# Four moved pieces in a two-block transformer kernel: which weight quarter is loaded first, when gated results are transposed, when the seven-product blocks start, and which PSUM banks the mixers' transposes use

## The chip, the cores and the metric

One core of one Trainium2 chip runs the whole program. The metric is the device time of one execution in microseconds. The kernel before took 1137.19 us (median of 3 runs, 1135.1 to 1139.62).

## What is computed

Two transformer blocks on 256 tokens of width 1024, all in float32. Each block is a SwiGLU feed-forward network (FFN) of inner width 2816, a mixer (sparse attention with pooling in the first, spatial gating with short convolution in the second), and another FFN; a last normalisation follows. The part that the change touches most is the FFN, of which there are four:

```python
def swiglu(x, w_gate, w_up, w_down):
    return (jax.nn.silu(x @ w_gate) * (x @ w_up)) @ w_down

x = x + 0.5 * swiglu(rms_norm(x, ffn1_norm[l]), ffn1_w_gate[l], ffn1_w_up[l], ffn1_w_down[l])
x = x + mixer(rms_norm(x, mix_norm[l]))          # attention and pooling, or gating and convolution
x = x + 0.5 * swiglu(rms_norm(x, ffn2_norm[l]), ffn2_w_gate[l], ffn2_w_up[l], ffn2_w_down[l])
```

## The kernel before

**Products in three passes.** Each float32 operand is split into a high half (ACT, a rounding copy, L77) and a low half (DVE, the remainder, L78), and a product is three matmuls, high x high, low x high and high x low (`mm3`, L83 to L85). Every weight chunk of 128x2048 thus goes from a buffer in which a transfer lands (`raw`, two buffers, filled by SP's queue, L67; or `block`, four buffers in an FFN, filled by Pool's queue, L151) through ACT and DVE into one of three pairs `whi`/`wlo`, and then to TensorE (PE).

**An FFN's steps.** The gate and up weights are cut into pieces of 512 columns, j = 0 to 5 (piece 5 holds 256 columns of each). Pieces 0, 2, 4 and 5 take the plain way (`eight`, L344): a step is one chunk of 1 MB from SP's queue and 24 matmuls for the two token tiles. Piece 5 has two steps (letter e), pieces 2 and 4 four each (letters 2 and 4). Pieces 1 and 3 (`seven`, L358, with `quad`, L154) replace eight block products by seven: letters a and b, seven steps of 12 matmuls each. Below, a1 is the first step of a, 2.1 the first of piece 2, and so on. The `down` steps (letter d) take 24 matmuls (12 for chunk 5), in the order of chunks 0, 1, 2, 4, 5, 3 for the first half of the columns. The string `ORDER` is the order in which the steps are written into the program, for all four FFNs.

**The seven products.** `quad` loads four quarters w11, w12, w22 and w21 of the piece through Pool's queue. Step a2 wants w12+b22 and step a5 wants w11+b12. The sums are made by the transfer itself: a second transfer with `accum_op=add` (L175) goes into the same buffer. For w12 it waits until the first transfer has landed; for w11 also until a1's halves are made. For a6 and a7, DVE adds w22 and w21 to that block (L192, L195). Pool's queue is in order: a transfer whose buffer is not free holds up those behind it. The block buffers w22 and w21 get are those in which DVE combines the activations beforehand (`combined`, L133); the second of them is free only when the combined activations `xc` have been split.

**Work that is put off.** When a piece's gate and up results are done, DVE multiplies them into `pr` (L338), and `turned` (L204) transposes `pr` on PE (L210) and splits it into `act`, which the down steps read. `later(f, n)` keeps such a piece of work until n units have passed; `flush` after a step counts 1 unit for a step of a or b and 2 for any other (L408). With n = 2, `turned` comes right after the step that ended the piece (for piece 0, right after the next step).

**PSUM.** Of the eight banks five are called `acc` and three `tmp`. `bank` takes the next buffer of one name in turn; `ps` (L58) goes through all eight. In the mixers most tiles come from `ps`, but `turned` and the transposes of the next stage's input (`pair`, L266) take `tmp`. `spare` is true in the mixers alone.

A scheduler orders the instructions on each engine; the code order is its input.

Of the kernel before, what the change touches and what calls it, by code (L numbers as in the profile page):

```python
# [17 lines left out]
P = 128  # L18
T = 256
# [13 lines left out]
MASKED = -1.0e30  # L33
WARM = 14

ORDER = "eaeaa2a2aa2a244bb4bb4bdbdbdddddddddd"


class Block:
# [14 lines left out]

    def bank(self, tag, shape=(P, 512)):
        return self.psum.tile(list(shape), F32, tag=tag, name=tag, bufs={"acc": 5, "tmp": 3}[tag])

    def ps(self, shape=(P, 512)):  # L58
        self.banks += 1
        return self.bank("acc" if self.banks % 8 < 5 else "tmp", shape)  # L60
# [93 lines left out]
    def quad(self, pool, b, x, xc):  # L154


        nc, tt = self.nc, self.nc.vector.tensor_tensor
        of_x = lambda c, t: lambda k: self.both(x[:, 4 * c + k, :, t * P : t * P + P])
        of_xc = lambda i: lambda k: self.both(xc[:, 4 * i + k, :, :])

        def product(left, w):
            ps = self.bank("tmp")
            for k in range(4):
                c = slice(k * 512, k * 512 + 512)
                self.mm3(ps, left(k), (w[0][:, c], w[1][:, c]), k == 0, k == 3)
            return ps

        p = lambda tag: pool.tile([P, 512], F32, tag=tag, name=tag)

        def copy(ps, tag):  # L170
            y = p(tag)
            nc.scalar.activation(y, ps, AF.Copy)
            return y

        more = lambda w, src: nc.gpsimd.dma_start(w, src, accum_op=ALU.add)  # L175
        (b11, b12), (b21, b22) = b
        w11, w12, w22, w21 = self.block(b11), self.block(b12), self.block(b22), self.block(b21)
        more(w12, b22)
        y11 = copy(product(of_x(0, 0), self.parts(w11)), "p1")
        more(w11, b12)  # L180
        yield
        p7 = copy(product(of_xc(2), self.parts(w12)), "p7")
        yield
        y12 = copy(product(of_xc(3), self.parts(w22)), "p3")
        yield
        y21 = p("p2")
        tt(y21, product(of_x(1, 0), self.parts(w21)), y11, op=ALU.add)
        y11, v = y21, y11
        yield
        p5 = copy(product(of_xc(0), self.parts(w11)), "p5")  # L190
        yield
        tt(w11, w11, w22, op=ALU.add)  # L192
        tt(v, product(of_xc(1), self.parts(w11)), v, op=ALU.subtract)
        yield
        tt(w11, w11, w21, op=ALU.add)  # L195
        w = self.parts(w11)
        ps = product(of_x(1, 1), w)
        tt(p7, p7, v, op=ALU.add)
        tt(v, v, p5, op=ALU.add)
        tt(p5, p7, p5, op=ALU.add)  # L200
        tt(p7, ps, p7, op=ALU.subtract)
        return y11, p7, y12, v, p5

    def turned(self, dst, x, k):  # L204

        for t in range(2):
            n = x[t].shape[1] // P
            pt = self.bank("tmp", (P, 4, P))
            for i in range(n):
                self.nc.tensor.transpose(pt[:, i, :], x[t][:, i * P : i * P + P], self.ident)  # L210
            s = slice(t * P, t * P + P)
            self.split(dst[:, k : k + n, 0, s], dst[:, k : k + n, 1, s], pt[:, :n, :])
# [37 lines left out]
    def add(self, accs, f, scale, following, tiles=(0, 1)):  # L250

        nc = self.nc
        s = slice(f * 512, f * 512 + 512)
        for t in tiles:
            x = self.X[t][:, s]
            nc.vector.scalar_tensor_tensor(x, accs[t], scale, x, op0=ALU.mult, op1=ALU.add)
        if following is None:
            return
        for t in tiles:
            self.squares(t, f)  # L260
        if following == "final_norm_2":
            return
        if f == 0:
            self.hT = self.big.tile([P, KD, 2, T], F32R, tag="hT", name="hT")

        def pair(k):  # L266
            pt = self.bank("tmp", (P, 2, T))
            for i in range(2):
                for t in range(2):
                    nc.tensor.transpose(pt[:, i, t * P : t * P + P], self.X[t][:, (k + i) * P : (k + i) * P + P], self.ident)  # L270
            for i in range(2):
                self.feed(k + i, pt[:, i, :], following)

        for k in (4 * f, 4 * f + 2):
            self.later(lambda k=k: pair(k), 3)
# [42 lines left out]
    def ffn(self, n, following, first=False):  # L318
        nc, a = self.nc, self.a
        gu, d, d_end = a[f"gu{n}"], a[f"d{n}"], a[f"de{n}"]  # L320
        with self.stage(4), self.tc.tile_pool(name="act", bufs=1) as pool:
            act = pool.tile([P, KF, 2, T], F32R, tag="act", name="act")
# [11 lines left out]
            def gated(j, sgs, us):  # L334
                prs = []
                for t in range(2):
                    pr = self.work.tile([P, 512], F32, tag="pr", name="pr", bufs=4)[:, : us[t].shape[1]]
                    nc.vector.scalar_tensor_tensor(pr, us[t], r[:, t : t + 1], sgs[t], op0=ALU.mult, op1=ALU.mult)  # L338
                    prs.append(pr)
                self.later(lambda: self.turned(act, prs, 4 * j), 2)  # L340

            two = lambda: [self.bank("acc") for _ in range(2)]

            def eight(j):  # L344
                G = two()
                self.token_major(G, gu[2 * j], 512, 0)
                yield
                self.token_major(G, gu[2 * j], 512, 1)
                sgs = silu([x[:, :T] for x in G] if j == 5 else G)
                if j < 5:  # L350
                    yield
                    U = two()
                    self.token_major(U, gu[2 * j + 1], 512, 0)
                    yield
                    self.token_major(U, gu[2 * j + 1], 512, 1)
                gated(j, sgs, [x[:, T:] for x in G] if j == 5 else U)

            def seven(j):  # L358
                y11, y21, y12, x, y22 = yield from self.quad(pool, [[gu[2 * j + i, c] for i in range(2)] for c in range(2)], self.hT, xc)

                def rest():
                    tt = nc.vector.tensor_tensor
                    tt(y12, y12, x, op=ALU.add)
                    gated(j, silu([y11, y21]), [y12, y22])

                self.later(rest, 3)

            def down():
                for f in range(2):
                    accs = two()  # L370
                    w = lambda c: self.weights(d[f, c] if c < 5 else d_end[f])
                    rows = lambda c, w, last, **k: self.rows(accs, w, act, 4 * c, 4 if c < 5 else 2, last, **k)
                    split = f == 1 and following == "final_norm_2"
                    order = (0, 1, 2, 4, 5, 3) if f == 0 else range(4 if split else 6)
                    for c in order:
                        if f or c:
                            yield
                        rows(c, w(c), 15 if f == 0 else KF - 1)
                    if split:
                        ws = [w(4), w(5)]  # L380
                        for t in range(2):
                            for c in (4, 5):
                                rows(c, ws[c - 4], KF - 1, tiles=[t])
                            self.add(accs, f, 0.5, following, [t])
                    else:
                        self.add(accs, f, 0.5, following)
# [12 lines left out]
            if not first:  # L399
                self.token_major(U, gu[1], 512, 1)  # L400
            gated(0, silu(G), U)
            combined = self.combined(xc, self.hT)
            next(combined)

            steps = {"a": seven(1), "b": seven(3), "2": eight(2), "4": eight(4), "e": eight(5), "d": down()}
            for step in ORDER:
                next(steps[step], None)
# [34 lines left out]
    def mixer1(self, following):  # L442
# [225 lines left out]
        def out(t, O):  # L668
# [4 lines left out]
            self.split(mT[0][:, :, 0, s], mT[0][:, :, 1, s], pt)  # L673

        ET = turned(0)
        pls = means()
        O = attend(0, ET)
        pooled(pls)
        ET = turned(1)
        mT[0] = self.m1.tile([P, 4, 2, T], F32R, tag="L1", name="mT")  # L680
        project(1, 0)
# [281 lines left out]
```

## Time and profile before

| what | value |
|---|---|
| median of 3 runs | 1137.19 us (1135.1 to 1139.62) |
| profiled execution, its own time | 1135.03 us |
| its span, first to last instruction | 1133.3 us |
| PE busy | 1081.6 us, 95% of the span |
| DVE busy | 758.3 us, 67% |
| ACT busy | 576.0 us, 51% |
| mean granted TensorE clock | 0.983 of full speed |
| DMA engines' mean busy share, first two queues | 39.8% and 16.1% |

The profile comes from one execution. "Busy" counts instructions of an engine; the waits are in a view that says, for each group of instructions, what ended the idle time before them. The granted clock says at which of its two levels (1.2 and 2.4 GHz) TensorE ran in a stretch.

### The profile page before, as it was taken

Reading aid. Unit: us, or ns where it says so; the run is one execution under the profiler, and the core shown is the slowest. Engines: PE = TensorE matmul, PEld = TensorE weight load, DVE = VectorE, ACT = ScalarE, POOL = GpSimd, SP = SyncE. Lnnn points to the kernel's source line nnn. Section 1 sums busy time; section 2 is a strip of 40 time slices with the busy share of each in tenths; the row PEclk is TensorE's granted clock in tenths of the full one; section 3 lists DMA queues with packets and bytes.
Section 4 is the critical chain, followed back from the end, with each engine's and each line's share of the span. In section 5 each row is a group of like instructions: output and inputs, shape, how many; then the busy total and the mean of one; then the engine's idle time right before and its main releaser. Section 6 shows DMA issues by size and latency. Waiting matters only on the chain.

```text
span 1133.3 us, 12907 instructions
## 1 busy us (share of the span) xinstructions
PE 1081.6 (95%) x5182; PEld 900.8 (79%) x5182; DVE 758.3 (67%) x780; ACT 576.0 (51%) x657; POOL 51.2 (5%) x85
## 2 busy tenths in 40 slices
PE   9898999899998899999889999999999999889996
PEld 7677888778887688888768878999888878767885
DVE  6685875597575769646776855687545557666953
ACT  7545543577454464544646454533444445546442
POOL 1100000120010000001000000000000001000000
PEclk9999999999998999999989999999999999999999
DMA  9956365633386743659574565454545438674362
GB/s 355 284 176 226 112 231 187 251 112 113 112 290 192 259 115 132 224 188 313 179 260 112 206 229 208 175 189 174 184 176 178 169 120 281 201 253 119 130 223 74
DMA packets 34956, 218.54 MB, mean 193 GB/s; under 512 B 4609, under 2 KB 5009, under 8 KB 10321
## 3 DMA queue, kind: packets, MB, share of 16 engines
q1 hardware_dynamic: 26784, 164.20, 39.8%
q0 software_dynamic: 7680, 52.98, 16.1%
q8 instruction: 40, 0.66, 0.2%
q10 hardware_dynamic: 432, 0.55, 0.1%
q14 instruction: 20, 0.16, 0.0%
HBM read 216.66 MB, written 1.05 MB: 192 GB/s over the span
## 4 chain that ended last, share of the span: by engine, by line
PE 70%; DVE 10%; DMA 10%; issue 5%; ACT 4%; POOL 0%; SPq 0%; POOLq 0%; ACTq 0%; DVEq 0%
PE acc L85 16%; PE acc L83 16%; PE acc L84 16%; PE tmp L83 6%; PE tmp L84 6%; PE tmp L85 6%; DVE wlo L78 6%; DMA block<-in_gu 5%; DMA raw<-in_gu 4%; ACT whi L77 3%; PE tmp L210 2%; PE acc L91 1%; DMA raw<-in_d 1%; DVE xc L78 1%; DVE block L192 1%
## 5 line engine op out<-in xcount | busy, mean ns | idle before, releaser
L78 DVE TENSOR_TENSOR wlo<-raw,whi 128x2048 fp32r<-128x2048 f32 (+1 forms) x127 | 282.2, 2222 | 175.4 <-ACT whi L77 175.4
L77 ACT ACTIVATE whi<-raw 128x2048 fp32r<-128x2048 f32 (+1 forms) x127 | 236.3, 1860 | 244.3 <-PE acc L85 106.8
L78 DVE TENSOR_TENSOR wlo<-block,whi 128x2048 fp32r<-128x2048 f32 (+2 forms) x99 | 198.5, 2013 | 100.4 <-ACT whi L77 100.3
L85 PE MATMUL acc<-whi,hT 128*128 128x512 f32 (+1 forms) x608 | 238.1, 392 | 3.2 <-DVE hT L223 3.2
L83 PE MATMUL acc<-whi,hT 128*128 128x512 f32 (+1 forms) x608 | 240.0, 396 | 0.5 <-ACT whi L77 0.4
L84 PE MATMUL acc<-wlo,hT 128*128 128x512 f32 (+1 forms) x608 | 238.4, 392 | 1.3 <-DVE wlo L78 1.3
L77 ACT ACTIVATE whi<-block 128x2048 fp32r<-128x2048 f32 (+2 forms) x99 | 166.7, 1691 | 107.5 <-PE acc L85 27.3
L84 PE MATMUL acc<-wlo,act 128*128 128x512 f32 x352 | 137.1, 389 | 0.6 <-DVE wlo L78 0.6
L83 PE MATMUL acc<-whi,act 128*128 128x512 f32 x352 | 137.6, 391 | 0.0
L85 PEld LDWEIGHTS acc<-whi,hT 128*128 128x128 f32 x608 | 115.8, 190 | 27.0 <-DVE hT L223 3.6
L85 PE MATMUL acc<-whi,act 128*128 128x512 f32 x352 | 136.9, 392 | 0.1
L84 PEld LDWEIGHTS acc<-wlo,hT 128*128 128x128 f32 x608 | 116.0, 191 | 24.6 <-DVE wlo L78 2.1
L83 PEld LDWEIGHTS acc<-whi,hT 128*128 128x128 f32 x608 | 116.2, 191 | 24.3 <-ACT hT L222 0.8
L85 PEld LDWEIGHTS acc<-whi,act 128*128 128x128 f32 x352 | 66.1, 188 | 15.2 <-DVE act L78 1.6
L84 PEld LDWEIGHTS acc<-wlo,act 128*128 128x128 f32 x352 | 66.1, 188 | 14.6 <-DVE wlo L78 1.0
L83 PEld LDWEIGHTS acc<-whi,act 128*128 128x128 f32 x352 | 66.1, 188 | 13.3
L83 PE MATMUL tmp<-whi,hT 128*128 128x512 f32 x144 | 57.2, 397 | 4.3 <-ACT whi L77 4.3
L84 PE MATMUL tmp<-wlo,hT 128*128 128x512 f32 x144 | 56.2, 390 | 0.0
L85 PE MATMUL tmp<-whi,hT 128*128 128x512 f32 x144 | 56.1, 390 | 0.0
L84 PE MATMUL tmp<-wlo,xc 128*128 128x512 f32 x128 | 52.7, 412 | 1.6 <-DVE wlo L78 1.6
L83 PE MATMUL tmp<-whi,xc 128*128 128x512 f32 x128 | 53.5, 418 | 0.0
L210 PE MATMUL tmp<-ident,pr 128*128 128x128 f32 x176 | 27.9, 296 | 26.6 <-DVE pr L338 26.6
(249 smaller groups left out, 1390.6 us busy)
## 6 DMA issues: line engine op xcount, KB each, us to landing
raw<-in_gu SPq DMA_DIRECT2D x52, 1024.0 KB, 4.9
block<-in_gu POOLq DMA_DIRECT2D x48, 1024.0 KB, 8.5
raw<-in_d SPq DMA_DIRECT2D x40, 1024.0 KB, 4.8
raw<-in_de SPq DMA_DIRECT2D x8, 512.0 KB, 3.5
block<-in_w_out SPq DMA_DIRECT2D x4, 1024.0 KB, 4.9
raw<-in_w_out SPq DMA_DIRECT2D x4, 1024.0 KB, 5.1
block<-in_w_cx SPq DMA_DIRECT2D x4, 1024.0 KB, 4.9
raw<-in_w_cx SPq DMA_DIRECT2D x4, 1024.0 KB, 5.0
```

The lines of the kernel that those rows point to most:

```text
L77: self.nc.scalar.activation(hi, x, AF.Copy)
L78: self.nc.vector.tensor_tensor(lo, x, hi.bitcast(F32), op=ALU.subtract)
L83: mm(ps, lhsT=a[0], rhs=b[0], start=start, stop=False)
L84: mm(ps, lhsT=a[0], rhs=b[1], start=False, stop=False)
L85: mm(ps, lhsT=a[1], rhs=b[0], start=False, stop=stop)
L91: self.nc.tensor.matmul(ps, lhsT=a, rhs=b, start=start, stop=stop)
L192: tt(w11, w11, w22, op=ALU.add)
L210: self.nc.tensor.transpose(pt[:, i, :], x[t][:, i * P : i * P + P], self.ident)
```

## The change

Four edits. (1) In `quad`, w12 is asked for before w11, and its accumulating transfer is written directly behind it, ahead of the loads of w11, w22 and w21. (2) `turned` of a gated piece is put off by 4 units and not 2, so it comes one plain step or two product steps later. (3) `ORDER`: the first part was e1 a1 e2 a2 a3 2.1 a4 2.2 a5 a6 2.3 a7 2.4 and is e1 e2 a1 a2 2.1 a3 2.2 a4 a5 2.3 a6 2.4 a7; in b, b4 and b5 are neighbours where b3 and b4 were. (4) In the mixers `turned` and `pair` take their banks from `ps`, all eight in turn; in the FFNs they take `tmp` as before.

```diff
-ORDER = "eaeaa2a2aa2a244bb4bb4bdbdbdddddddddd"
+ORDER = "eeaa2a2aa2a2a44bb4b4bbdbdbdddddddddd"

+    def side(self, shape):
+        return self.ps(shape) if self.spare else self.bank("tmp", shape)

         (b11, b12), (b21, b22) = b
-        w11, w12, w22, w21 = self.block(b11), self.block(b12), self.block(b22), self.block(b21)
+        w12 = self.block(b12)
         more(w12, b22)
+        w11, w22, w21 = self.block(b11), self.block(b22), self.block(b21)
         y11 = copy(product(of_x(0, 0), self.parts(w11)), "p1")
...
-            pt = self.bank("tmp", (P, 4, P))
+            pt = self.side((P, 4, P))
...
-            pt = self.bank("tmp", (P, 2, T))
+            pt = self.side((P, 2, T))
...
-                self.later(lambda: self.turned(act, prs, 4 * j), 2)
+                self.later(lambda: self.turned(act, prs, 4 * j), 4)
```

In the program that is built from it, the engines' rows move as follows (line numbers of the changed file are 3 or 4 higher).

Pool's queue at the start of the second FFN, before: 2687 is w11, 2689 is w12, 2691 and 2693 are w22 and w21; L175 is the accumulating transfer; 3116 and 3118 are w11 and w12 of piece 3.

```order
L151 DMA block_2687<-in_gu2 128x2048
L151 DMA block_2689<-in_gu2 128x2048
L151 DMA block_2691<-in_gu2 128x2048
L151 DMA block_2693<-in_gu2 128x2048
L175 DMA block_2689<-in_gu2 128x2048
L175 DMA block_2687<-in_gu2 128x2048
L151 DMA block_3116<-in_gu2 128x2048
L151 DMA block_3118<-in_gu2 128x2048
L175 DMA block_3118<-in_gu2 128x2048
```

The same place after: 2725 is w12, 2728 w11, 2730 and 2732 are w22 and w21; 3102 is w12 of piece 3, and 3105 its w11.

```order
L154 DMA block_2725<-in_gu2 128x2048
L154 DMA block_2728<-in_gu2 128x2048
L178 DMA block_2725<-in_gu2 128x2048
L154 DMA block_2730<-in_gu2 128x2048
L154 DMA block_2732<-in_gu2 128x2048
L178 DMA block_2728<-in_gu2 128x2048
L154 DMA block_3102<-in_gu2 128x2048
L178 DMA block_3102<-in_gu2 128x2048
L154 DMA block_3105<-in_gu2 128x2048
```

The first accumulating transfer moved from behind w21's load to ahead of w22's; in piece 3 it moved ahead of w11's load.

DVE at the start of the second FFN, before: the combined activations (`xc`), the gated results of piece 0 (pr_2628, pr_2630) and of piece 5 (pr_2750, pr_2752), and the low halves of w11 (2697), of e2's chunk (2719), of w12 (2765) and of w22 (2784).

```order
L338 SCALAR_TENSOR_TENSOR pr_2628<-acc_2478,rstd_2590,sg_2624 128x512
L78 TENSOR_TENSOR xc_2475<-block_2634,xc_2475 128x16x128
L338 SCALAR_TENSOR_TENSOR pr_2630<-acc_2479,rstd_2590,sg_2626 128x512
L78 TENSOR_TENSOR wlo_2697<-block_2687,whi_2696 128x2048
L78 TENSOR_TENSOR wlo_2719<-raw_2716,whi_2718 128x2048
L78 TENSOR_TENSOR act_2474<-tmp_2671,act_2474 128x4x128
L78 TENSOR_TENSOR act_2474<-tmp_2678,act_2474 128x4x128
L78 TENSOR_TENSOR wlo_2765<-block_2689,whi_2764 128x2048
L338 SCALAR_TENSOR_TENSOR pr_2750<-acc_2639,rstd_2590,sg_2746 128x256
L338 SCALAR_TENSOR_TENSOR pr_2752<-acc_2640,rstd_2590,sg_2748 128x256
L78 TENSOR_TENSOR wlo_2784<-block_2691,whi_2783 128x2048
```

The same place after: 2676 is the low half of e2's chunk, 2735 of w11, 2755 of w12, 2788 of the chunk of step 2.1; pr_2707 and pr_2709 are piece 5's.

```order
L81 TENSOR_TENSOR wlo_2676<-raw_2673,whi_2675 128x2048
L342 SCALAR_TENSOR_TENSOR pr_2628<-acc_2478,rstd_2590,sg_2624 128x512
L81 TENSOR_TENSOR xc_2475<-block_2634,xc_2475 128x16x128
L342 SCALAR_TENSOR_TENSOR pr_2630<-acc_2479,rstd_2590,sg_2626 128x512
L81 TENSOR_TENSOR wlo_2735<-block_2728,whi_2734 128x2048
L81 TENSOR_TENSOR wlo_2755<-block_2725,whi_2754 128x2048
L342 SCALAR_TENSOR_TENSOR pr_2707<-acc_2639,rstd_2590,sg_2703 128x256
L342 SCALAR_TENSOR_TENSOR pr_2709<-acc_2640,rstd_2590,sg_2705 128x256
L81 TENSOR_TENSOR wlo_2788<-raw_2785,whi_2787 128x2048
L81 TENSOR_TENSOR act_2474<-tmp_2711,act_2474 128x4x128
L81 TENSOR_TENSOR act_2474<-tmp_2718,act_2474 128x4x128
```

e2's chunk moved to the front, w12's low half still stands ahead of piece 5's gated results, and the split of piece 0's transposes moved behind all of them.

DVE at a5 to a7 of the second FFN, before: 2888 is a5's low half, L192 and L195 the two additions, 2908 a6's low half, 2930 that of step 2.3's chunk, 2959 a7's.

```order
L78 TENSOR_TENSOR wlo_2888<-block_2687,whi_2887 128x2048
L187 TENSOR_TENSOR p2_2834<-tmp_2839,p1_2713 128x512
L192 TENSOR_TENSOR block_2687<-block_2687,block_2691 128x2048
L78 TENSOR_TENSOR wlo_2908<-block_2687,whi_2907 128x2048
L195 TENSOR_TENSOR block_2687<-block_2687,block_2693 128x2048
L78 TENSOR_TENSOR wlo_2930<-raw_2927,whi_2929 128x2048
L193 TENSOR_TENSOR p1_2713<-tmp_2911,p1_2713 128x512
L78 TENSOR_TENSOR wlo_2959<-block_2687,whi_2958 128x2048
```

The same place after: the additions are L196 and L199; 2911 is the low half of step 2.3's chunk, 2940 a6's, 2960 that of step 2.4's chunk, 2993 a7's.

```order
L81 TENSOR_TENSOR wlo_2888<-block_2728,whi_2887 128x2048
L196 TENSOR_TENSOR block_2728<-block_2728,block_2730 128x2048
L81 TENSOR_TENSOR wlo_2911<-raw_2908,whi_2910 128x2048
L191 TENSOR_TENSOR p2_2868<-tmp_2873,p1_2751 128x512
L81 TENSOR_TENSOR wlo_2940<-block_2728,whi_2939 128x2048
L199 TENSOR_TENSOR block_2728<-block_2728,block_2732 128x2048
L81 TENSOR_TENSOR wlo_2960<-raw_2957,whi_2959 128x2048
L81 TENSOR_TENSOR wlo_2993<-block_2728,whi_2992 128x2048
```

A plain chunk's low half moved in between each addition and the split of its sum, as a plain step now lies between a5, a6 and a7 on PE.

## Rows read from the trace of the kernel before

**Rows 1.** The page's first part: busy time of PE (share of the span, instructions) and of the other engines.

```profile
PE 1081.6 (95%) x5182; PEld 900.8 (79%) x5182; DVE 758.3 (67%) x780; ACT 576.0 (51%) x657; POOL 51.2 (5%) x85
```

**Rows 2.** The view of waits, PE alone, whole span: which instructions waited, for what, us in total, times, longest. `pr` is a gated result, tmp products are steps of a and b, mT belongs to the mixers, hT to a stage's input.

```profile
PE tmp L210 <- DVE pr L338: 26.6, 10, 4.1
PE tmp L83 <- ACT whi L77: 4.3, 4, 1.1
PE acc L85 <- DVE hT L223: 3.2, 1, 3.2
PE acc L84 <- DVE wlo L78: 1.9, 3, 1.1
PE tmp L84 <- DVE wlo L78: 1.6, 4, 0.4
PE acc L83 <- ACT mT L77: 1.6, 1, 1.6
PE acc L85 <- DVE mT L78: 1.2, 1, 1.2
```

**Rows 3.** The view of stretches, for the seven stretches of the FFNs (after the first 10 us) in which the granted clock was half, first and last of the seven with the sum of all; then a stretch of the second FFN for comparison. Columns: the stretch, its length, busy us (instructions) of PE, weight loads, DVE, ACT, POOL, then the granted clock, the DMA engines' busy share and GB/s.

```profile
50.00:53.40 3.40, 3.40 (x10) 2.72 (x10) 3.40 (x4) 1.56 (x2) 0.23 (x1) 0.50 0.69 243
...
971.60:975.00 3.40, 2.79 (x9) 2.30 (x10) 3.40 (x6) 2.71 (x4) 0.55 (x1) 0.50 0.84 222
sum 30.70, PE 28.34 PEld 22.34 DVE 25.88 ACT 20.86 POOL 1.69; mean PE 4.05 PEld 3.19 DVE 3.70 ACT 2.98 POOL 0.24
354.00:394.70 40.70, 37.09 (x163) 29.86 (x162) 27.51 (x18) 19.34 (x14) 2.49 (x4) 1.00 0.63 214
```

**Rows 4.** PE's instructions in order of time, second FFN (start, us, instruction; in brackets the idle time before it and what ended it): the end of e1 and piece 0's transposes, the four waits, and two neighbouring matmuls.

```profile
335.51 0.71 PE L210 MATMUL tmp<-ident,pr 128*128 128x128 f32 x5
...
347.95 1.12 PE L210 MATMUL tmp<-ident,pr 128*128 128x128 f32 x4 [3.23 <-DVE pr L338]
...
373.83 0.50 PE L84 MATMUL tmp<-wlo,xc 128*128 128x512 f32 x1 [0.41 <-DVE wlo L78]
...
378.17 0.51 PE L83 MATMUL tmp<-whi,hT 128*128 128x512 f32 x1 [1.07 <-ACT whi L77]
...
391.02 0.39 PE L84 MATMUL acc<-wlo,hT 128*128 128x512 f32 x1
391.25 0.39 PE L85 MATMUL acc<-whi,hT 128*128 128x512 f32 x1
393.77 0.66 PE L210 MATMUL tmp<-ident,pr 128*128 128x128 f32 x4 [2.13 <-DVE pr L338]
```

**Rows 5.** ACT's and DVE's instructions in order of time just before the wait that ended at 347.95: the split of w12, and piece 5's gated results behind it.

```profile
343.25 1.92 ACT L77 ACTIVATE whi<-block 128x2048 fp32r<-128x2048 f32 x1 [3.34 <-DMA block<-in_gu]
345.20 2.29 DVE L78 TENSOR_TENSOR wlo<-block,whi 128x2048 fp32r<-128x2048 f32 x1 [7.14 <-ACT whi L77]
347.41 0.87 DVE L338 SCALAR_TENSOR_TENSOR pr<-acc,rstd,sg 128x256 f32<-128x256 f32 x2
```

**Rows 6.** Pool's instructions at the start of the second FFN: the loads of w11 and w12 (one row, x2), of w22, of w21, and w12's accumulating transfer (L175).

```profile
313.32 1.13 POOL L151 DMA_DIRECT2D block<-in_gu  x2 [0.25 <-issue]
326.45 0.53 POOL L151 DMA_DIRECT2D block<-in_gu  x1 [12.00 <-DVE block L144]
330.86 0.53 POOL L151 DMA_DIRECT2D block<-in_gu  x1 [3.87 <-DVE xc L78]
331.37 0.93 POOL L175 DMA_DIRECT2D block<-in_gu  x1
```

**Rows 7.** Times from issue to landing: two rows of the page's list of issues (median us at the end), the line on the sixteen accumulating transfers from the view of L175, and three transfers of the chain that ended last (start, us, what): w12's second transfer in the first FFN and in the second, and the chunk of step 4.1 in the second.

```profile
raw<-in_gu SPq DMA_DIRECT2D x52, 1024.0 KB, 4.9
block<-in_gu POOLq DMA_DIRECT2D x48, 1024.0 KB, 8.5
...
DMA to landing us min/median/max: 7.7/10.6/17.6
...
31.55 13.56 DMA block<-in_gu
...
331.37 11.80 DMA block<-in_gu
...
378.34 9.77 DMA raw<-in_gu
```

**Rows 8.** DVE's first addition for a6 and ACT's split of the sum, and ACT's copy of a product step's result (second FFN, in order of time).

```profile
339.31 0.60 ACT L172 ACTIVATE p<-tmp 128x512 f32<-128x512 f32 x1 [2.08 <-PE tmp L85]
...
367.16 2.28 DVE L192 TENSOR_TENSOR block<-block 128x2048 f32<-128x2048 f32 x1
369.54 1.92 ACT L77 ACTIVATE whi<-block 128x2048 fp32r<-128x2048 f32 x1 [1.05 <-DVE block L192]
```

**Rows 9.** First FFN, instructions in order of time: ACT's split of the quarter that Pool's first load brought, and PE's first matmul of e1 that needed a low half.

```profile
28.02 1.90 ACT L77 ACTIVATE whi<-block 128x2048 fp32r<-128x2048 f32 x1
...
30.90 0.50 PE L84 MATMUL acc<-wlo,hT 128*128 128x512 f32 x1 [1.11 <-DVE wlo L78]
```

**Rows 10.** DVE's low half of step 4.1's chunk in the second FFN, just before the wait that ended at 393.77.

```profile
390.16 2.29 DVE L78 TENSOR_TENSOR wlo<-raw,whi 128x2048 fp32r<-128x2048 f32 x1 [4.32 <-ACT whi L77]
```

**Rows 11.** Second FFN, before the last down chunk of the first half: PE's transposes of piece 3, and DVE's split of them.

```profile
460.77 1.04 PE L210 MATMUL tmp<-ident,pr 128*128 128x128 f32 x8
...
465.18 1.28 DVE L78 TENSOR_TENSOR act<-tmp,act 128x512 fp32r<-128x512 f32 x2
```

## Prediction

> **What bounds the kernel now.** I read the page's busy times first: PE is busy 95% of the span, no other engine over 67% [rows 1], so only what keeps PE idle or slow counts. The view of waits names it: PE waits 26.6 us in ten places for a gated result `pr` before transposing it, 4.3 us for the high half and 1.6 us for the low half of a product step's weights, four times each, which is once per FFN [rows 2]: 32.5 us, all inside the FFNs. Then the stretches: behind the waits the granted clock is 0.50, that is 1.2 instead of 2.4 GHz, in seven stretches of 30.7 us together, in which PE was busy 28.34 us [rows 3]; work done there takes twice its time, so 14.2 us are lost. With them the FFNs lose 46.7 us of the span of 1133.3.
>
> The second FFN shows why. PE's row at 347.95 waited 3.23 us for `pr` [rows 4]. That `pr` (347.41) stood on DVE behind the low half of w12 (345.20), this behind ACT's high half (343.25), which waited for the transfer [rows 5]. Pool asked for w12's accumulating transfer at 331.37, though w12 had been asked for at 313.32: it stood behind w21's load, which waited for DVE's split of `xc` until 330.86 [rows 6]. It then took 11.80 us [rows 7]. So PE, transposing something else, waits for a weight quarter through DVE's order. Two shorter waits (0.41 and 1.07 us) follow at a6 and a7, and one of 2.13 us at 393.77 for piece 2's `pr` [rows 4].
>
> **Part by part.** Two neighbouring matmuls start 0.23 us apart at full clock [rows 4]: a plain step of 24 takes 5.5 us, a product step of 12 takes 2.75, and a wait of 0.4 us is two matmuls.
>
> *w12 first.* After the change e2 follows e1, which ended at 335.5 [rows 4]: e2 to 341.0, piece 0's transposes (1.04 for eight, as in [rows 11]) to 342.0, a1 to 344.8, two matmuls of step 2.1, and a2 is due at 345.2. w12's load is asked for at 313.3 and lands after 8.5 us, the accumulating transfer after another 10.6 (7.7 to 17.6) [rows 7]: 332.4, at worst 339.4. High and low half take 1.92 and 2.29 us [rows 5]: ready at 336.6, at worst 343.6, before 345.2. Weight buffers don't hold it up either: the pair it takes is e1's, free at 335.5, which makes 339.7. The wait of 3.23 us goes, and its like in the third and fourth FFN. The first FFN is tighter: Pool's first load was split at 28.02 [rows 9], so w12 lands by then; plus 10.6 and 4.2 us makes 42.8, with the 13.56 seen there [rows 7] 45.8. a2 is due at 30.9 [rows 9] plus 11.0 for e1 and e2, 1.0, 2.75 and 0.4: 46.1. I take nothing for it; with 17.6 us PE waits 3.7. What Pool's queue is moved past: w11's load still goes out before the queue stops for w12's landing; w22's load is now behind that stop (some 322), but its buffer was free only at 326.45 [rows 6], so it loses nothing, and a1's quarter still has 28 us until a1.
>
> *a6 and a7.* DVE's addition takes 2.28 us, ACT starts 0.1 us later [rows 8], the halves take 4.2: 6.6 us from a5's split to a6's weights. Between a5 and a6 stood nothing, now a plain step does, and between a6 and a7 too: 5.5 plus the product's 2.75 make 8.25. The cover exceeds the chain by 1.7 us; I take both waits (0.41 and 1.07) as gone. If a plain chunk's low half (2.29) comes ahead of a6's on DVE, as the order of DVE now has it, 0.6 us stay; that is the upper end.
>
> *Transposes later.* Piece 2's `pr` was missed by 2.13 us; now step 4.1 (5.5 us) lies between. What is late next is step 4.1's own chunk: its low half ended at 392.45 [rows 10], and PE got there at 391.6, so if nothing else moved 0.6 us would stay per FFN. The chunk had taken 9.77 us to land, against a median of 4.9 [rows 7]. It is now asked for earlier, since the raw buffer it needs is released by step 2.3's split, which stands ahead of L195 instead of behind it, and piece 3's w12 with its accumulation has gone out by then. I take it as gone; both ends 0 and 2.13. Four of the ten waits for `pr` are w12's, four of this kind, and the two left (first and fourth FFN) follow these and go with the same delay.
>
> *What the delay costs.* Piece 3's transposes now come after down chunk 5, right before chunk 3, which reads them. Before, DVE had written the first tile's low half at 465.8 (465.18 plus half of 1.28), 4.0 us after the transposes ended [rows 11], because a weight split stood ahead of it. That split starts when chunk 4's buffers come free, which is now 2.75 us earlier against the transposes: 1.3 us remain, and the six matmuls that PE has in hand take 1.4. Cost 0.1 per FFN; without that shift 2.7.
>
> *A new wait.* In the built program a1 and a2 use the same PSUM bank in every FFN (`tmp` has three, piece 0's two transposes hold the others). a2 must wait until ACT has copied a1's result, 0.60 us [rows 8], with 0.45 us of step 2.1 to cover it; at worst a high half (1.92) is ahead on ACT. I take 0.5 per FFN, at most 2.1: 2.0 us in all, at most 8.4.
>
> *The mixers' banks.* At the end of the second mixer PE waits 1.6 and 1.2 us for its transposed result [rows 2]. With the next half's accumulators no longer in `tmp`, the scheduler puts up to 16 of their matmuls into these waits: 2.5 of 2.8 us. Elsewhere in the mixers a bank in turn may be taken or freed later; no row prices that, so 0, within plus or minus 2, as large as this gain. The wait for hT in the first mixer (3.2) and three for low halves (1.9) [rows 2] are untouched.
>
> **Sum.** Against the profiled execution's 1135.03: minus 32.5, minus 14.2 (no long wait, so no half clock), minus 2.5, plus 2.0, plus 0.4 is 1088.2. The median of the runs is 2.2 above this execution: 1090.4. I say 1090.5. With all FFN losses gone and no costs it would be 1086; with the mixers better too, 1083.
>
> **Against it: the clock.** Waits of 0.41 and 1.07 us lie in a stretch of 40.7 us with a granted clock of 1.00 [rows 3, 4]; the stretches of 0.50 follow longer ones, as that of 347.0 to 353.8, one of the seven, follows the 3.23. The Trainium skill, "TensorE: Matmul & The Clock Gate", section "A second HAM failure mode: psum-queue depth-cycling", says otherwise: short idle moments between groups of matmuls, as PSUM banks are cycled, can by themselves throw the clock back and forth. By that rule the new bank waits at a2 would keep the half clock though the long waits go. Such a mechanism would leave the 14.2 us of the seven stretches in place: 1104.6. The row with clock 1.00 speaks against it.
>
> **Rivals.** (1) *The waits move.* w12 stays late in the first FFN (3.7), 0.6 us stay at a6 and 2.13 at step 4.1 (10.9 in four FFNs), the bank wait is 2.1 (6.4 more), piece 3 costs 2.7 (10.4 more); half of this is 15.7, and half of the clock loss stays with it, 7.1: 1113. For it: DVE's order still puts w12 ahead of piece 5's `pr`; against it: the margins above. (2) *The clock stays* as above: 1104.6. (3) *The change does not do what it says:* the transfers are the limit. From 354 to 394.7 the DMA engines were busy 0.63 of the time at 214 GB/s [rows 3]; if accumulating transfers allow no more, the gate and up steps cannot be done faster and the time stays at 1137. Against it: one stretch of the rows shows 0.84, and in that of 0.63 the loads wait for buffers. (4) *Slower: SP's two raw buffers.* A buffer's round is landing plus 4.2 us, and PE uses a plain chunk in 5.5; two buffers keep up while landing stays below 6.8. Accumulating transfers now run beside e2's and piece 2's chunks. If all 14 gate and up chunks landed after 9.77 us, as the one did, each would come (9.77+4.2)/2-5.5 = 1.5 us late: 84 us over four FFNs, 47 of it paid by the gain: 1174. It decides where the mean landing passes 8.5 us, (12.7/2-5.5) x 56 = 47.6. Against it: the median of 4.9 includes many chunks beside Pool's loads, and between product steps chunks are used more slowly than one in 5.5.
>
> **How the numbers follow.** Forecast (1083 to 1102) 0.72; waits move 0.16; clock stays 0.05; no change 0.03; slower 0.04. The range 1081 to 1113 leaves out the last two, half of the second and a little below: under 2 in 10. About 0.5% is what a measurement of this kernel can tell from no change (5.7 us): faster than 1131.5 in the first three cases, 0.93; same 0.03; slower 0.04.
>
> **What would show it.** Right: PE's waits for `pr` fall from 26.6 to under 5 us, those of a product step's L83 and L84 for whi and wlo too; mean clock above 0.99; w12's accumulation is asked for before 325 in the second FFN. New rows: a2's first matmul waiting for ACT's copy (L172 before), and chunk 3 of the down steps for act. Wrong: a2 waiting for w12's whi, raw chunks landing after 8 us or more, or half clock without a long wait.

## The result and the profile after

The changed kernel takes 1084.74 us (median of 4 runs, 1084.13 to 1086.12), the kernel before 1137.11 in 4 runs beside it: ratio 0.954, 95% interval 0.9519 to 0.9561, 52.4 us less. In the changed kernel's code, lines 58 to 178 of before stand 3 lower and those behind them 4 lower: L78 is L81, L172 is L175, L175 is L178, L210 is L214. The profiled execution took 1086.12 us; its span is 49.0 us shorter than before. One execution of less_banks, a kernel described below, ran at a mean granted clock of 0.556 and took 1791.87 us; it is left out of that kernel's median.

The page's first row (answers to [rows 1]):

```profile
PE 1064.9 (98%) x5182; PEld 893.0 (82%) x5182; DVE 758.4 (70%) x780; ACT 576.4 (53%) x657; POOL 51.0 (5%) x85
```

The same instructions on every engine; PE is busy 16.7 us less, since more of its work runs at full clock, and the rest of the 49.0 is idle time that is gone. The view of waits, PE alone (answers to [rows 2]):

```profile
PE acc L87 <- DVE wlo L81: 3.7, 3, 1.7
PE acc L88 <- DVE hT L227: 3.2, 1, 3.2
PE tmp L86 <- ACT p L175: 1.0, 4, 0.3
PE tmp L94 <- POOL mhalf L838: 1.0, 1, 1.0
PE tmp L94 <- ACT rel L498: 0.7, 1, 0.7
PE acc L86 <- ACT whi L80: 0.5, 1, 0.5
```

The row for `pr`, 26.6 us before, is not there any more, nor are those of a product step's weights (4.3 and 1.6) and of mT (1.6 and 1.2): 35.3 us. New are a2's wait for ACT's copy (1.0 in four FFNs) and a wait for `rel` in the first mixer (0.7). The waits for low halves of SP's chunks grew from 1.9 to 3.7, and the row for a high half, `PE acc L83 <- ACT whi L77: 0.4, 1, 0.4` before, is 0.5 now, at another place.

The view of stretches, with the columns of [rows 3]: the only stretch at half clock between the first 10 us and the last 7 (in which PE has no instruction), which stands in the first mixer at the wait of 3.2 us for hT, and 92 us of the second FFN.

```profile
203.90:210.70 6.80, 5.58 (x20) 5.34 (x21) 5.34 (x10) 3.19 (x4) 0.00 (x0) 0.50 0.67 245
320.00:412.00 92.00, 91.77 (x423) 76.02 (x422) 73.02 (x52) 55.57 (x50) 5.30 (x8) 1.00 0.65 214
```

All seven stretches of the FFNs are gone; in the second FFN PE is busy for 91.77 of 92.00 us. The mixer's stretch is an eighth that the kernel before has too, at the same wait for hT, but there it is half as long (a row of before):

```profile
217.26:220.67 3.41, 3.41 (x14) 3.24 (x13) 2.10 (x3) 2.32 (x2) 0.00 (x0) 0.50 0.74 281
```

PE in order of time, second FFN (answers to [rows 4]): a2's first matmul with the new wait, the transposes of piece 5 (for whose `pr` PE waited 3.23 us before), the first two matmuls of a6 and of a7, and the transposes of piece 2 (2.13 us before).

```profile
334.66 0.50 PE L86 MATMUL tmp<-whi,xc 128*128 128x512 f32 x1 [0.23 <-ACT p L175]
...
337.52 0.60 PE L214 MATMUL tmp<-ident,pr 128*128 128x128 f32 x4
...
362.02 0.39 PE L86 MATMUL tmp<-whi,xc 128*128 128x512 f32 x1
362.24 0.39 PE L87 MATMUL tmp<-wlo,xc 128*128 128x512 f32 x1
...
370.18 0.39 PE L86 MATMUL tmp<-whi,hT 128*128 128x512 f32 x1
370.40 0.39 PE L87 MATMUL tmp<-wlo,hT 128*128 128x512 f32 x1
...
378.34 1.03 PE L214 MATMUL tmp<-ident,pr 128*128 128x128 f32 x8
```

No bracket means no idle time before the row: a6, a7 and the transposes now find their operands. Pool, ACT and DVE at the start of the second FFN, with w12's split on ACT and DVE (answers to [rows 5, 6]):

```profile
302.61 1.13 POOL L154 DMA_DIRECT2D block<-in_gu  x2 [0.25 <-issue]
309.61 0.88 POOL L178 DMA_DIRECT2D block<-in_gu  x1 [5.87 <-DMA block<-in_gu]
315.71 0.55 POOL L154 DMA_DIRECT2D block<-in_gu  x1 [5.22 <-DVE block L147]
322.80 0.53 POOL L154 DMA_DIRECT2D block<-in_gu  x1 [6.55 <-DVE xc L81]
...
325.00 1.92 ACT L80 ACTIVATE whi<-block 128x2048 fp32r<-128x2048 f32 x1 [3.52 <-PE acc L88]
...
326.95 2.29 DVE L81 TENSOR_TENSOR wlo<-block,whi 128x2048 fp32r<-128x2048 f32 x1 [1.59 <-ACT whi L80]
```

w12's accumulating transfer (L178) now goes out 7.0 us after the first loads, as soon as w12 has landed, and no more 18 us after them behind w21's load. ACT's split of w12 at 325.00 waited for PE to free a weight buffer, not for a transfer; its low half was ready at 329.24, and a2 came at 334.43. One row of the list of issues and the line on accumulating transfers (answer to [rows 7]):

```profile
raw<-in_gu SPq DMA_DIRECT2D x52, 1024.0 KB, 6.7
...
DMA to landing us min/median/max: 7.7/9.4/14.6
```

The median landing of SP's chunks is 6.7 us instead of 4.9; what that median hides is in the last section. One chunk does cost time: in the first FFN, e2's now has to be there straight behind e1's. It landed 15.2 us after it was asked for (13.7 before, where a1's weights were split ahead of it), and ACT and then PE waited:

```profile
30.86 1.92 ACT L80 ACTIVATE whi<-raw 128x2048 fp32r<-128x2048 f32 x1 [2.76 <-DMA raw<-in_gu]
...
35.16 0.50 PE L87 MATMUL acc<-wlo,hT 128*128 128x512 f32 x1 [1.62 <-DVE wlo L81]
```

### The profile page after: what moved, and what is told of

The parts are those of the page before. It is cut to its first block, busy times and chain, and to the rows that moved or that the text cites. A ratio compares the mean times of both kernels' runs of the same rounds, so it can differ in the third digit from the quotient of the medians.

```text
span 1084.3 us, 12898 instructions
## 1 busy us (share of the span) xinstructions
PE 1064.9 (98%) x5182; PEld 893.0 (82%) x5182; DVE 758.4 (70%) x780; ACT 576.4 (53%) x657; POOL 51.0 (5%) x85
## 3 DMA queue, kind: packets, MB, share of 16 engines
q0 software_dynamic: 7680, 52.98, 16.7%
## 4 chain that ended last, share of the span: by engine, by line
PE 92%; DMA 5%; DVE 1%; ACT 1%; issue 1%; SPq 0%; POOLq 0%; POOL 0%; ACTq 0%; DVEq 0%
PE acc L88 21%; PE acc L87 21%; PE acc L86 20%; PE tmp L86 8%; PE tmp L88 8%; PE tmp L87 8%; PE tmp L214 2%; DMA raw<-in_gu 1%; PE acc L94 1%; DMA block<-in_gu 1%; DVE wlo L81 1%; DMA qg<-in_q_norm 1%; DMA raw<-in_de 1%; PE tmp L274 1%; PE tmp L94 1%
## 5 line engine op out<-in xcount | busy, mean ns | idle before, releaser
L81 DVE TENSOR_TENSOR wlo<-raw,whi 128x2048 fp32r<-128x2048 f32 (+1 forms) x127 | 282.2, 2222 | 157.2 <-ACT whi L80 156.9
L81 DVE TENSOR_TENSOR wlo<-block,whi 128x2048 fp32r<-128x2048 f32 (+2 forms) x99 | 198.8, 2014 | 71.4 <-ACT whi L80 71.4
L87 PE MATMUL acc<-wlo,hT 128*128 128x512 f32 (+1 forms) x560 | 218.6, 390 | 3.3 <-DVE wlo L81 3.3
L88 PE MATMUL acc<-whi,hT 128*128 128x512 f32 (+1 forms) x560 | 218.0, 390 | 3.2 <-DVE hT L227 3.2
L86 PE MATMUL acc<-whi,hT 128*128 128x512 f32 (+1 forms) x560 | 218.8, 392 | 0.0
L87 PEld LDWEIGHTS acc<-wlo,hT 128*128 128x128 f32 x560 | 106.1, 189 | 25.5 <-DVE wlo L81 4.4
L88 PEld LDWEIGHTS acc<-whi,hT 128*128 128x128 f32 x560 | 106.1, 189 | 24.6 <-DVE hT L227 3.5
L86 PEld LDWEIGHTS acc<-whi,hT 128*128 128x128 f32 x560 | 106.2, 190 | 21.9 <-ACT hT L226 0.5
L86 PE MATMUL tmp<-whi,hT 128*128 128x512 f32 x192 | 75.8, 395 | 0.0
L88 PE MATMUL tmp<-whi,hT 128*128 128x512 f32 x192 | 74.8, 390 | 0.0
L87 PE MATMUL tmp<-wlo,hT 128*128 128x512 f32 x192 | 74.8, 389 | 0.0
L86 PE MATMUL tmp<-whi,xc 128*128 128x512 f32 x128 | 50.2, 392 | 1.0 <-ACT p L175 1.0
L88 PE MATMUL tmp<-whi,xc 128*128 128x512 f32 x128 | 49.9, 390 | 0.0
L87 PE MATMUL tmp<-wlo,xc 128*128 128x512 f32 x128 | 49.8, 389 | 0.0
```

Source lines behind the costliest of these rows:

```text
L81: self.nc.vector.tensor_tensor(lo, x, hi.bitcast(F32), op=ALU.subtract)
L86: mm(ps, lhsT=a[0], rhs=b[0], start=start, stop=False)
L87: mm(ps, lhsT=a[0], rhs=b[1], start=False, stop=False)
L88: mm(ps, lhsT=a[1], rhs=b[0], start=False, stop=stop)
```

## The experiments

**Theory.** w12's accumulating transfer, queued behind w21's load, is the root of the longest waits; transposing too early makes the next ones; the order of steps covers a6 and a7; half clock follows the long waits and goes with them. **Rival:** one edit alone (the order, which gives w12 5.5 us more, or the delay) would have been enough, or the clock falls for another reason. Each edit was made alone in the kernel before (only_), and taken back alone from the changed kernel (less_).

| kernel | median us | ratio to before, 95% interval | gained or given back, us |
|---|---|---|---|
| only_quarter | 1114.40 | 0.9792 (0.9766 to 0.9818) | 23.4 gained |
| only_delay | 1128.92 | 0.9912 (0.9881 to 0.9944) | 8.9 gained |
| only_order | 1135.59 | 0.9990 (0.9967 to 1.0013) | 2.2 gained, or nothing |
| only_banks | 1132.46 | 0.9947 (0.9927 to 0.9967) | 5.4 gained |
| less_quarter | 1108.75 | 0.9731 (0.9696 to 0.9766) | 24.0 given back |
| less_delay | 1096.71 | 0.9633 (0.9609 to 0.9657) | 12.0 given back |
| less_order | 1099.14 | 0.9661 (0.9631 to 0.9692) | 14.4 given back |
| less_banks | 1086.94 | 0.9556 (0.9532 to 0.9580) | 2.2 given back, or nothing |
| sum_last | 1111.20 | 0.9769 (0.9740 to 0.9798) | 26.5 given back |
| pool_tables | 1080.08 | 0.9495 (0.9469 to 0.9522) | 4.7 gained on the changed kernel |

The last column is the median of before beside the only_ kernels (1137.82) less each of them, and for the others the difference to 1084.74. The four edits alone sum to 39.9 us, together they give 52.4. The less_ kernels ran beside executions of before with a median of 1139.27, 2.2 us above those beside the changed kernel (1137.11), so a difference of that size in their rows can't be told from nothing: the interval of less_banks overlaps that of the changed kernel (0.9519 to 0.9561).

### The first edit alone, and without it

```
- w11, w12, w22, w21 = self.block(b11), self.block(b12), self.block(b22), self.block(b21)
+ w12 = self.block(b12)
  more(w12, b22)
+ w11, w22, w21 = self.block(b11), self.block(b22), self.block(b21)
```

> The kernel before with the load order of the four quarters alone (w12 and its accumulating transfer first). Theory: the four longest waits of the transposes for pr come from w12 landing behind w21; they go (13.6 us), and with them the half-clock stretches that follow them (about 8 us): some 1116 us. The waits of about 1 us before a6 and a7, and those of the transposes one step after the gating, stay. Rival: the transfer was hidden by the order of steps or another load takes its place, and nothing moves: 1137 us.

Measured: 1114.40. The view of waits of this kernel:

```profile
PE tmp L211 <- DVE pr L339: 10.8, 9, 2.6
PE tmp L83 <- ACT whi L77: 4.6, 4, 1.4
```

Of 26.6 us for `pr` 15.8 are gone, and the waits at a6 and a7 stay, as the theory had it.

> The changed kernel with the old load order of the quarters (w12 behind w11, its accumulation behind w21's load). Theory: w12 is complete some 10 us later and a2 waits for it, 2 to 3 us in each of three or four FFNs, with some clock lost after the longest: 1092 to 1100 us. Rival: the steps of e2 ahead of a and the later transposes leave enough time, and it stays at 1085 us.

Measured: 1108.75. The theory's sign, but 24.0 us where it allowed 15 at most: PE waits for w12 at a2 in the first and third FFN (2.5 and 2.1 us), and in the second and fourth longer, 3.75 and 5.3 us, for a plain chunk. Why a plain chunk, the next kernel shows.

### The order of steps alone, and without it

```
-ORDER = "eaeaa2a2aa2a244bb4bb4bdbdbdddddddddd"
+ORDER = "eeaa2a2aa2a2a44bb4b4bbdbdbdddddddddd"
```

> The kernel before with the new order of steps alone (e2 ahead of the first a step, a6 and a7 later). Theory: the waits before a6 and a7 go (6 us) and the w12 transfer has one step of 5.5 us more, which shortens the four long waits only in part, and the transposes of the early gating still wait: 1119 to 1135 us. Rival: the 5.5 us more is what w12 needed, and the long waits go too: 1105 to 1112 us.

Measured: 1135.59, no change that the interval can tell. The theory's range just misses it and its reason fails: `pr` is hardly waited for any more (1.6 us), but PE waits 27.0 us for high halves of SP's chunks, 21.8 of it in one wait of 2.1 to 7.3 us in each FFN. PE and ACT in the second FFN, and from the view of the accumulating transfers' line who waited for them:

```profile
345.31 0.80 PE L83 MATMUL acc<-whi,hT 128*128 128x512 f32 x1 [5.90 <-ACT whi L77]
...
340.91 1.91 ACT L77 ACTIVATE whi<-block 128x2048 fp32r<-128x2048 f32 x1 [3.89 <-DMA block<-in_gu]
342.73 0.46 ACT L330 ACTIVATE sg<-acc,rstd 128x256 f32<-128x256 f32 x1
343.08 0.37 ACT L77 ACTIVATE act<-tmp 128x256 fp32r<-128x256 f32 x1
343.35 1.91 ACT L77 ACTIVATE whi<-raw 128x2048 fp32r<-128x2048 f32 x1
...
  ACT whi L77: 14.0, 4
```

ACT stands 3.89 us at w12, which is still in transfer, and the chunk of step 2.1, which came through SP's queue and not Pool's, is split behind it at 343.35. PE is at step 2.1 from 339.4 and idles for 5.9 us. So the late quarter stops whoever is queued behind it: before, a gated result on DVE; here, a plain chunk on ACT. Moving steps only changes who that is.

> The changed kernel with the old order of steps. Theory: the waits before a6 and a7 come back (6 us in four FFNs), w12 with its early load is in time: 1091 us. Rival: a2 stands one step earlier and waits for w12 again, with clock lost: 1100 us or more.

Measured: 1099.14; neither the theory's 1091 nor the rival's reason. In this profile (1096.58 us, the shortest of four executions) a7 waits 4.3 us and a6 1.4 in four FFNs, nearly the 6 us expected, a2 does not wait for w12, but a1 of the first FFN waits 4.3 us:

```profile
33.63 0.50 PE L86 MATMUL tmp<-whi,hT 128*128 128x512 f32 x1 [4.30 <-ACT whi L80]
...
31.67 1.91 ACT L80 ACTIVATE whi<-block 128x2048 fp32r<-128x2048 f32 x1 [2.93 <-DMA block<-in_gu]
```

ACT waits there for w11, which is now loaded second. Loading w12 first has a price in the first FFN, where nothing was loaded ahead; e2 ahead of a1 hides it. That is one piece of what the edits give only together. Of the 14.4 us these two kinds of waits are 10.0; the rest stays open.

### The later transposes alone, and without them

```
- self.later(lambda: self.turned(act, prs, 4 * j), 2)
+ self.later(lambda: self.turned(act, prs, 4 * j), 4)
```

> The kernel before with the later turn of the gated results alone (4 in place of 2). Theory: the transposes no longer stand in TensorE's queue before pr is there; the waits on pr go in all FFNs (24 us), but where w12 is late a wait of 2 to 3 us at a2 takes their place, since the transfer still lands late: 1117 to 1120 us, with half-clock stretches left in FFN2 to FFN4. Rival: the delay is all that mattered, and a2 finds w12 in time: 1096 us or less.

Measured: 1128.92. The place is as expected, the size is not: `pr` costs 1.2 us, and w12's lateness appears at a2 (third FFN, the two waits together 2.8 us); but PE then waits for step 4.1's low half too, 1.8 us in the fourth FFN (the last row) and 1.7 in the third, and the mean granted clock stays at 0.982 (0.983 before). In the view of waits 25.4 us for `pr` are gone, and the waits for weights grew by 19.1, from 8.2 to 27.3.

```profile
533.26 0.51 PE L83 MATMUL tmp<-whi,xc 128*128 128x512 f32 x1 [0.98 <-ACT whi L77]
535.59 0.50 PE L84 MATMUL tmp<-wlo,xc 128*128 128x512 f32 x1 [1.82 <-DVE wlo L78]
...
1014.15 0.80 PE L84 MATMUL acc<-wlo,hT 128*128 128x512 f32 x1 [1.82 <-DVE wlo L78]
```

> The changed kernel with the transposes of the gated results two steps after the gating, as before. Theory: TensorE stands at the transposes until pr is there, 1 to 2 us for several pieces of each FFN, and loses clock behind the longest: 1097 to 1106 us. Rival: with w12 early DVE is never behind, and the transposes find pr: 1085 us.

Measured: 1096.71, just below the theory's range; `PE tmp L214 <- DVE pr L342` is back with 4.8 us in eight waits, and PE waits 5.6 us for high halves, 1.3 of it at a down step in each FFN. So early transposes cost time even when w12 is in time, but not where the prediction had them: the waits for `pr` are 0.9 to 1.4 us at piece 5's transposes in each FFN, and there is none at piece 2's (2.1 to 3.2 us in each FFN before).

### The mixers' banks alone, and without them

```
- pt = self.bank("tmp", (P, 4, P))
+ pt = self.side((P, 4, P))
...
- pt = self.bank("tmp", (P, 2, T))
+ pt = self.side((P, 2, T))
```

> The kernel before with the alternating banks of the mixers' transposes alone. Theory: only the two waits for mT in the second mixer go (2.8 us): 1134 us, FFNs as before. Rival: the scheduler's order of the mixers changes with the banks, and a new wait eats it: 1137 us.

> The changed kernel with the mixers' transposes all in the tmp banks. Theory: the second mixer's waits for mT come back: 1087.5 us (2.8 us more). Rival: no difference, since the waits belonged to the order of the steps: 1085 us.

Measured: 1132.46 and 1086.94, 5.4 and 2.2 us, the second not clear of nothing. Without the edit the two waits are back in the view of waits of less_banks, with the numbers of before:

```profile
PE acc L86 <- ACT mT L80: 1.6, 1, 1.6
PE acc L88 <- DVE mT L81: 1.2, 1, 1.2
```

The rows give 2.8 less 0.7 for `rel` in the first mixer, which comes with the edit (it is in only_banks, too). What the 5.4 of only_banks holds beyond that stays open: its profiled execution (1136.59) is the longest of its runs and does not show the gain.

The profiled execution of less_banks (1091.7 us) is the longest of its five, and at these two waits its granted clock falls to half:

```profile
879.10:885.90 6.80, 6.01 (x14) 4.77 (x15) 2.02 (x4) 0.61 (x2) 0.00 (x0) 0.50 0.46 157
```

In the kernel before, the same two waits (the second ends at 914.87) are followed by full clock:

```profile
914.00:921.00 7.00, 6.13 (x27) 5.03 (x28) 2.80 (x5) 1.91 (x3) 0.00 (x0) 1.00 0.43 152
```

So waits of 1.6 and 1.2 us are followed by half clock in one trace and not in the other; no run here shows what decides it.

### The place of the accumulating transfer

Here w12 is loaded first as in the changed kernel, but its accumulating transfer goes out behind the other three loads.

```
  w12 = self.block(b12)
- more(w12, b22)
  w11, w22, w21 = self.block(b11), self.block(b22), self.block(b21)
+ more(w12, b22)
```

> The changed kernel with w12 still loaded first, but its accumulating transfer issued after the loads of w11, w22 and w21. Theory: not the place of w12's load but the place of the accumulation behind w21's load (which waits for a free block) is what made w12 late; ScalarE's split of w12 then waits for the transfer again and the chunk behind it waits too, 2 to 5 us in three or four FFNs and the clock behind them: 1100 to 1112 us, near the kernel without the first edit (1108.8 us). Rival: with its load first w12 is early enough, or the load of w12 itself was the late part: 1085 to 1090 us.

Measured: 1111.20, as far off as without the first edit at all (their intervals overlap). Pool, ACT and PE in the second FFN, and who waited for the accumulating transfers:

```profile
306.46 1.13 POOL L154 DMA_DIRECT2D block<-in_gu  x2 [0.25 <-issue]
319.57 0.53 POOL L154 DMA_DIRECT2D block<-in_gu  x1 [11.98 <-DVE block L147]
325.90 0.53 POOL L154 DMA_DIRECT2D block<-in_gu  x1 [5.80 <-DVE xc L81]
326.42 0.93 POOL L178 DMA_DIRECT2D block<-in_gu  x1
...
336.98 1.91 ACT L80 ACTIVATE whi<-block 128x2048 fp32r<-128x2048 f32 x1 [2.20 <-DMA block<-in_gu]
...
341.71 0.50 PE L86 MATMUL acc<-whi,hT 128*128 128x512 f32 x1 [3.88 <-ACT whi L80]
...
  ACT whi L80: 8.0, 3
```

The load of w12 went out at 306.46 and its accumulation 20 us later, held by two loads that waited for free blocks. In the changed kernel and in only_quarter no engine but Pool itself waits for an accumulating transfer. So in the changed kernel the whole of the first edit's gain is this place in Pool's queue.

### The wait that is left

In the changed kernel DVE stands 4.54 us at the first mixer's tables for `q_norm`, and hT's halves, which PE needs, are behind it (a row of the changed kernel):

```profile
201.43 0.29 DVE L440 TENSOR_TENSOR qC<-cosq,qg 128x128 f32<-128x128 f32 x1 [4.54 <-DMA qg<-in_q_norm]
```

Here GpSimd multiplies the tables.

```
- nc.vector.tensor_tensor(C, cosq, g[:, None, :].to_broadcast([P, 2, HD]), op=ALU.mult)
+ nc.gpsimd.tensor_tensor(C, cosq, g[:, None, :].to_broadcast([P, 2, HD]), op=ALU.mult)
...
- nc.vector.tensor_tensor(S[:, :, o], sinq[:, :, o], g[:, None, s].to_broadcast([P, 2, 32]), op=ALU.mult)
+ nc.gpsimd.tensor_tensor(S[:, :, o], sinq[:, :, o], g[:, None, s].to_broadcast([P, 2, 32]), op=ALU.mult)
```

> The changed kernel with the first mixer's four tables (qC, qS, kC, kS) multiplied on GpSimd in place of VectorE, so that VectorE does not wait for the loads of the norms ahead of hT. Theory: the wait of TensorE for hT (3.2 us), the longest that is left, goes or falls under 1 us, and with it the only half-clock stretch (2.2 us above the normal pace): 1079 to 1081 us. Rival: the clock falls there whether TensorE waits or not, or GpSimd's tables are late for the heads: 1082 to 1086 us.

Measured: 1080.08 (1079.39 to 1080.54), as the theory had it, all runs below all of the changed kernel. GpSimd now waits for the load, and the first mixer's stretch runs at full clock (columns of [rows 3]):

```profile
200.93 0.46 POOL L440 TENSOR_TENSOR qC<-cosq,qg 128x128 f32<-128x128 f32 x1 [3.33 <-DMA qg<-in_q_norm]
...
200.00:206.00 6.00, 6.00 (x36) 5.59 (x35) 3.59 (x6) 3.88 (x6) 2.00 (x6) 1.00 1.01 417
```

The span is 6.0 us shorter. The wait itself was 3.2, and half of the 5.58 us in which PE was busy at half clock is 2.8.

## Why the prediction was right, step by step

- **What bounds the kernel, and w12 first.** Right, and shown by only_quarter, less_quarter and sum_last: Pool's queue held w12's accumulation, and ACT and DVE passed the delay on. The timing held in the second FFN: the split waited for e1's buffers and the low half was ready 5.2 us ahead of a2, forecast 5.5 (345.2 less 339.7). In the first FFN a2 waits only 0.23 us for ACT's copy.
- **The FFNs' waits, 32.5 us.** All gone. The prediction missed what the new order costs in the first FFN: PE now waits 1.7 and 1.6 us for the low halves of the e steps, where before it waited 1.1 once, and the second of these waits goes back to e2's chunk, which landed late. The row grew by 1.8.
- **Half clock, 14.2 us.** Gone as forecast: PE's busy time fell by 16.7 us, and the mean granted clock rose from 0.983 to 0.994. That the waits come first is shown by what went with them: the seven stretches with the FFNs' waits, the mixer's with the hT wait in pool_tables. Which waits the half clock follows is not settled: less_banks and before differ at the same two. The Trainium skill ("TensorE: Matmul & The Clock Gate", section "A second HAM failure mode: psum-queue depth-cycling") tells of a clock that goes back and forth because TensorE is idle for short moments between groups of matmuls as PSUM banks are cycled in every iteration. The trace shows no such effect of a2's bank wait, which comes once in each FFN: in the second it lies in 92 us of granted clock 1.00. Waits that come as often as the page has them are in no run here.
- **The new bank wait, 2.0 us.** It came at every a2, as the built order told, and took 0.23 to 0.33 us each: 1.0. ACT copied at once.
- **Transposes later, and a6 and a7.** The waits went, 5.9 us at a6 and a7, and 10.3 at piece 2's transposes. less_order brings a6's and a7's back (5.7). Piece 2's don't come back in less_delay: the order of steps had removed them too, since only_quarter keeps them (1.5 to 2.6 us each) and only_order does not (1.6 us for all `pr`). Here the prediction had the amount right, and put it down to one edit where two remove it.
- **Piece 3's late transposes, 0.4 us.** No wait for `act` is listed: 0.
- **The mixers' banks, 2.5 us.** By the rows 2.8 less 0.7; by less_banks 2.2, within what can't be told from nothing.
- **The sum.** By these rows: 35.3 gone, 3.6 new or grown (1.0 + 0.7 + 1.8 + 0.1), 14.2 of clock gone in the FFNs and 1.1 more lost in the first mixer (half of 5.58 less half of 3.41): 44.8 of the 49.0 us by which the span fell. The forecast was 46.8. The other 4.2 us belong to no row of these views. The rest of the difference between 1090.5 and 1084.74 lies in the runs: before, the median was 2.2 above the profiled execution, after, it is 1.4 below. That is luck, and the prediction's lower end needed it: its 1086 (no costs) and 1083 (better mixers) leave out the 2.2 that its forecast adds. With it they are 1088 and 1085, and the measured median is below both.
- **The rivals.** The waits did not move, but only_order shows that mechanism at its purest, with w12 still late. The transfers are not the limit: the gate and up steps run at PE's pace at the same 214 GB/s. For SP's raw chunks the fourth rival's limits, 6.8 and 8.5 us, are for the mean landing, and the prediction held the median of 4.9 against them. The mean of the 52 gate and up chunks was 6.76 before and is 6.95 after, so it stood near the first limit in both and the change hardly moved it. The sign "raw chunks landing after 8 us or more" separates nothing: 16 of the 52 did before, 14 do after.
- **What it did not see.** It took the edits as a sum. The order of steps is worth 2.2 us or nothing alone, because the late quarter then costs at step 2.1 what a6 and a7 give, and 14.4 on top of the others.

## What to carry to other kernels

When one engine waits, follow the queue of each engine back to a transfer before moving work: here moving steps alone gained nothing that can be told and moving transposes alone 8.9 of 52.4 us, since other work then stood behind the late quarter. On a queue that issues loads in order, put the transfer with the longest chain behind it (load, accumulate, split) ahead of loads that wait for free buffers. And try edits of this kind together, since the value of one can be hidden until another has removed the wait ahead of it.

## What was not expected of the hardware

A median can move where the transfers as a whole do not. The median landing of SP's 1 MB gate and up chunks is 4.9 us in each of the five kernels with the old load order (before, only_delay, only_order, only_banks, less_quarter), and 5.9 to 6.7 in the six with w12's accumulation early (only_quarter 6.5, less_delay 6.4, less_order 5.9, less_banks 6.5, pool_tables 6.1, the changed kernel 6.7); in sum_last it is 5.2. But the mean, worked out from the issue and the landing of each of the 52, is 6.76 before and 6.95 after, and between 6.3 and 7.0 in all twelve.

What moves the median is what a chunk shares its time with. In the kernel before, the median is 4.7 us for the 23 chunks with no transfer of Pool's queue beside them, 8.2 for the 12 that have a plain load (and no accumulating transfer) beside them for over half of their time, and 10.9 for the 9 that have an accumulating transfer there. In the changed kernel it is 4.7 (12 chunks), 7.2 (13) and 8.8 (15). More chunks now meet an accumulating transfer, and those that do land sooner. Why an accumulating transfer goes with the slowest landings was not tried.
